# A two-layer encoder on one core: the last down-projection made token-major, with seven half-size products in place of eight

## The chip, the core and the metric

The kernel runs on one core of a Trainium2 chip. The metric is device time in microseconds of one execution, input and output in the chip's memory. The engines named below are PE (TensorE: matmuls), ACT (ScalarE), DVE (VectorE), POOL (GpSimd) and SP (SyncE, which here only issues DMAs). SBUF is the on-chip memory of 128 partitions, PSUM the eight banks into which PE accumulates.

## The reference

A bidirectional encoder trunk of two layers, in float32, on 512 tokens of 1024 channels. Cut to what matters here:

```python
for l in range(DEPTH):                          # DEPTH = 2
    h = rmsnorm(x, g_mix[l])
    proj = h @ w_in[l]                          # gates, conv, three attentions
    ...                                         # four branches, gated and summed
    x = x + mixed @ w_out[l]
    x = x + conv_ffn(rmsnorm(x, g_ffn[l]), w_up[l], ffn_conv_w[l], ffn_conv_b[l], w_down[l])

def conv_ffn(h, w_up, conv_w, conv_b, w_down):
    u = depthwise_conv(h @ w_up, conv_w, conv_b)      # width 3 over the tokens
    gate, up = split(u, 2)                            # 2816 channels each
    return (silu(gate) * up) @ w_down                 # 2816 -> 1024
```

The output is x, 512 tokens by 1024 channels.

## The kernel before

**Products in three parts.** Matmuls run in the type float32r. To keep float32's precision each operand is split into a rounded part (hi) and a rest (lo), and each product is three matmuls, hi x hi, hi x lo and lo x hi, added up in one PSUM bank. A matmul takes a stationary operand of 128 x 128 and a moving one of 128 x 512, and writes 128 x 512, one bank. `prod` issues these three.

**Feature-major.** Mostly activations lie with channels on the partitions and tokens along the row, as blocks of 128 channels by 512 tokens; the weights are the stationary operand. The projections that feed attention are token-major (`token_major`): there the activations are stationary, 128 tokens at a time, and the weights move, 512 columns at a time.

**Weights.** They are packed on the host into units of up to 1024 columns of 128 partitions (512 KB), in order of use (`weight_units`, `pack_weights`). `weights` emits for each unit a DMA on SP's queue into `w_raw` (two buffers), a copy by ACT into `w_hi` and a subtraction by DVE into `w_lo` (three buffers each). `unit` hands out the next one. All instructions are put in order when the program is built: each has a priority, that of its place in the code, weights some 3000 places ahead of theirs, and an engine's queue takes what is ready in that plan, by priority. On the chip every engine then works its queue strictly in order. A buffer that is used again waits until all that used it before is done.

**The feed-forward part.** `ffn` takes 22 block pairs i; for each, two up-projection blocks of 24 matmuls (gate and up), then scaling, the convolution over tokens and the gating on DVE and ACT, in buffers `U0` to `U3`, `cy0`, `cy1` and `fth`, and at its end the split of the block into `fh` and `fl`, which stay. The down-projection then runs over eight output blocks m, each the sum over 22 blocks, with three weight units of 1024, 896 and 896 columns, and `update` adds the residual (`xr`, loaded from memory, to `xn`) and stores it; in the last layer into `outT`, feature-major, which the host transposes. In the first layer `update` also prepares the next layer's normalised input (`norm_tile`), and `finish_norm` starts the row of scales, which goes through memory on POOL's queue.

**PSUM.** Two groups of four banks in rotation, `mm` and `aux`; the feed-forward part uses `mm` alone.

**Memory pools.** `gate`, `attn`, `outp` and `ffn` are opened one after another in each layer and share SBUF; a buffer of a later pool waits for those that lay there before.

Of the kernel before, what the change touches and what calls it, by code (L numbers as in the profile page):

```python
# [14 lines left out]
F32 = mybir.dt.float32  # L15
# [3 lines left out]
ALU = mybir.AluOpType  # L19
# [8 lines left out]
NB = S // P  # L28
DFF = 2816
NF = DFF // P  # L30
EPS = 1e-6
BIG = 1e30
EB = 4
# [29 lines left out]
COL_A, COL_NA, COL_DIL, COL_SWA = 4096, 4608, 5376, 6144  # L63


def weight_units():

    units = []

    tok = lambda *cols: units.extend(('in_t', (cols, k, 2), 1024) for k in range(0, 8, 2))  # L70
    tok((COL_NA, 512))
    tok((COL_NA + 512, 256), (COL_DIL + 512, 256))
    tok((COL_DIL, 512))
    for j in (2, 0, 3, 1):
        units.append(('in_d', COL_A + j * P, 1024))
    tok((COL_SWA, 512))
    for n in ORDER:
        for d in range(8):
            units.append(('in_d', n * D + d * P, 1024))
            if d in (2, 6):  # L80
                units.append(('branch', (n, d // 4), 1024))
    for d in range(8):
        units.append(('out', d, 1024))
    for i in range(NF):
        units.append(('up', i * P, 1024))
        units.append(('up', DFF + i * P, 1024))
    for m in range(8):
# [5 lines left out]
UNITS = weight_units()  # L93
WLEN = sum(u[2] for u in UNITS) * P


def pack_weights(w_in, w_branch, w_out, w_up, w_down):
    out = np.empty((L, WLEN), np.float32)
    for l in range(L):
        off = 0  # L100
        for kind, a, n in UNITS:
            dst = out[l, off:off + n * P]
            off += n * P
            if kind == 'in_t':
                cols, k0, kn = a
                src = np.concatenate([w_in[l][k0 * P:(k0 + kn) * P, c:c + w] for c, w in cols], 1)
                src = src.reshape(kn, P, 512).transpose(1, 0, 2)
            elif kind == 'branch':
                b, h = a
                src = w_branch[l][b].reshape(2, P, 8, P)[:, :, 4 * h:4 * h + 4].transpose(1, 2, 0, 3)  # L110
            elif kind == 'down':
# [73 lines left out]
class Trunk:  # L185
# [7 lines left out]
    def weights(self, upto, ahead=3000, parts=1, queue=None):  # L193

        nc = self.nc
        while self.w_emitted < min(upto, len(self.w_list)):
            l, off, n = self.w_list[self.w_emitted]
            with self.tc.high_priority(offset=ahead):
                raw = self.wpool.tile([P, 1024], F32, name="w_raw", tag="w_raw", bufs=2)
                hi = self.wpool.tile([P, 1024], F32R, name="w_hi", tag="w_hi", bufs=3)  # L200
                lo = self.wpool.tile([P, 1024], F32R, name="w_lo", tag="w_lo", bufs=3)
                src = self.W[l, off:off + n * P].rearrange("(p c) -> p c", p=P)
                for i in range(parts):
                    s = slice(i * n // parts, (i + 1) * n // parts)
                    (queue or nc.sync).dma_start(raw[:, s], src[:, s])
                for i in range(parts):
                    s = slice(i * n // parts, (i + 1) * n // parts)
                    w = nc.scalar.activation(hi[:, s], raw[:, s], AF.Copy)  # L208
                    self.first_hi = self.first_hi or w
                    nc.vector.tensor_tensor(lo[:, s], raw[:, s], hi[:, s].bitcast(F32), ALU.subtract)  # L210
            self.w_ready.append((hi, lo))
            self.w_emitted += 1
# [7 lines left out]
    def mm(self):  # L220
        return self.psum.tile([P, 512], F32, name="mm", tag="mm", bufs=4)
# [610 lines left out]
            self.tick()  # L832


    def update(self, d, ps, pool, last):
# [5 lines left out]
        nc.vector.tensor_tensor(xn, ps, xr, ALU.add)  # L841
        if last:
            nc.sync.dma_start(self.out[d], xn)
        else:
            nc.sync.dma_start(self.xnew[d], xn)
            self.norm_tile(d, xn, pool)
# [5 lines left out]
    def ffn(self):  # L852
        nc = self.nc
        v = nc.vector
        U = []
        for i in range(4):
            u = self.fp.tile([P, 514 + (4 * PHASE if i == 3 else 0)], F32, name=f"U{i}", tag=f"U{i}", bufs=1)
            nc.gpsimd.memset(u[:, 0:1], 0.0)
            nc.gpsimd.memset(u[:, 513:514], 0.0)
            U.append(u)  # L860
        F = []
        for i in range(NF):
            ys, pss = [], []
            for s in range(2):
# [18 lines left out]
            f = ys[1]  # L883
            v.tensor_tensor(f, f, ys[0], ALU.mult)  # L884
            fh = self.fp.tile([P, S], F32R, name=f"fh{i}", tag=f"fh{i}", bufs=1)
            fl = self.fp.tile([P, S], F32R, name=f"fl{i}", tag=f"fl{i}", bufs=1)
            nc.scalar.activation(fh, f, AF.Copy, scale=0.5)  # L887
            v.scalar_tensor_tensor(fl, f, 0.5, fh.bitcast(F32), ALU.mult, ALU.subtract)
            F.append((fh, fl))
        return F  # L890


    def run(self):
        nc, tc = self.nc, self.tc
        with ExitStack() as st:
# [6 lines left out]
            self.dram = pool("dram", space=bass.MemoryType.DRAM)  # L902
            self.w_list = []
            for l in range(L):
                off = 0
                for _, _, n in UNITS:
                    self.w_list.append((l, off, n))
                    off += n * P
            self.w_emitted = self.w_used = 0
            self.first_hi = None  # L910
            self.w_ready = []
# [43 lines left out]
    def layer(self, l):  # L955
# [3 lines left out]
        with tc.tile_pool(name="gate", bufs=1, reuse_waits="tile") as self.gp:  # L959
# [26 lines left out]
            with tc.tile_pool(name="outp", bufs=1, reuse_waits="tile") as self.op:  # L986
# [3 lines left out]
                for d in range(0, KT, 2):  # L990
# [3 lines left out]
                    for k0, k1 in zip(cuts, cuts[1:]):  # L994
                        for e in range(2):
# [5 lines left out]
                                self.prod(pss[e], hi[:, s], lo[:, s], self.MH[k][0], self.MH[k][1], k == 0,  # L1001
                                          k == KT - 1)
                            if k1 == KT:
                                self.update(d + e, pss[e], self.op, False)
                self.xres = self.xnew
                self.finish_norm(1)
        with tc.tile_pool(name="ffn", bufs=1, reuse_waits="tile") as self.fp:
            self.scratch = lambda: self.fp.tile([P, S], F32, name="raw", tag="cy0", bufs=2)
            F = self.ffn()
            if not last:  # L1010
                self.load_prm(l + 1)
                self.xnew = self.new_res()
                self.start_norm('g_mix')
            for m in range(KT):
                ps = self.mm()
                for k0, kn in ((0, 8), (8, 7), (15, 7)):
                    hi, lo = self.unit()
                    for j in range(kn):
                        k = k0 + j
                        s = slice(j * P, (j + 1) * P)  # L1020
                        self.prod(ps, hi[:, s], lo[:, s], F[k][0], F[k][1], k == 0, k == NF - 1)
                self.update(m, ps, self.fp, last)
            if not last:
                self.xres = self.xnew
                self.finish_norm(1, 10)

    def derive_params(self):
        nc = self.nc
# [42 lines left out]
```

## Time and profile before

| | |
|---|---|
| time, median of 3 executions | 1587.83 us (1587.66 to 2181.0) |
| profiled execution | 1587.48 us, its span in the profile 1585.7 us |
| granted PE clock | 1.0 of full speed |
| matmuls | 7298 in the profile |
| first layer's down-projection | about 676 to 794 us |
| second layer's up-projection | about 1227 to 1461 us |
| last down-projection | 1461.7 to 1581.6 us |
| memory traffic | 177.70 MB, 112 GB/s in the mean |

The profile names instructions by line of the kernel, engine and operation, then the output and the inputs by the program's names (`mm<-fh,w_hi` is a matmul into an `mm` bank from these two), shapes, and a count. In the listings by line the figures after the bar are the time busy in all, the mean of one in ns, and the idle time of the engine just before them with what ended it. In the order of time each row starts with the start and the length in us. Times to landing are of a DMA from its issue to its completion. The line numbers are those of the kernel before.

### The profile page before, as it was taken

What the parts mean: (1) busy time and instruction counts of PE and PEld (TensorE: products, weight loads), DVE (VectorE), ACT (ScalarE), POOL (GpSimd) and SP (SyncE); (2) the same over time, 40 slices, a digit from 0 to 9 for tenths busy, and PEclk for the clock granted to TensorE, in tenths of its full rate; (3) what the DMA queues carried; (4) which work ended last, traced back from release to release, by engine and by line L of the source; (5) the groups of instructions that cost most, each with busy time, mean ns of one, the idle gap of its engine ahead of it and who ended that gap; (6) DMA issues with size and microseconds to landing.
All of it is one profiled execution on the core that took longest, in us unless ns stands there. A gap on an engine that the chain in (4) does not pass through costs nothing.

```text
span 1585.7 us, 19717 instructions
## 1 busy us (share of the span) xinstructions
PE 1579.1 (100%) x7298; PEld 1314.2 (83%) x7298; DVE 1103.3 (70%) x1847; ACT 782.0 (49%) x1334; POOL 105.6 (7%) x176
## 2 busy tenths in 40 slices
PE   9999999999999999999999999999999999999998
PEld 8888888888888888888888888888888888888887
DVE  6689888755578787743356898887556787787221
ACT  6778777243444444422247687763334444444221
POOL 0102001221000000000002020021210000000000
PEclk9999999999999999999999999999999999999999
DMA  6622222222532222234345312222326222222332
GB/s 236 184 97 89 85 80 76 98 100 98 183 118 98 102 93 94 103 118 139 118 157 174 111 68 86 79 86 90 104 94 211 93 107 99 94 94 101 123 130 71
DMA packets 60080, 177.70 MB, mean 112 GB/s; under 512 B 7120, under 2 KB 9040, under 8 KB 59984
## 3 DMA queue, kind: packets, MB, share of 16 engines
q1 hardware_dynamic: 59248, 174.87, 32.6%
q0 software_dynamic: 448, 1.06, 0.3%
q8 instruction: 57, 0.93, 0.2%
q10 hardware_dynamic: 288, 0.52, 0.1%
q14 instruction: 39, 0.32, 0.1%
HBM read 160.68 MB, written 10.49 MB: 108 GB/s over the span
## 4 chain that ended last, share of the span: by engine, by line
PE 94%; DVE 3%; ACT 3%; issue 0%; DMA 0%; SPq 0%; ACTq 0%; DVEq 0%
PE mm L231 26%; PE mm L229 26%; PE mm L230 26%; PE mm L423 2%; PE mm L425 2%; PE mm L424 2%; PE aux L695 2%; PE aux L424 1%; PE aux L425 1%; PE aux L423 1%; PE aux L657 1%; PE aux L658 1%; PE aux L719 1%; DVE w_lo L210 1%; ACT w_hi L208 1%; PE aux L722 0%
## 5 line engine op out<-in xcount | busy, mean ns | idle before, releaser
L229 PE MATMUL mm<-xh,w_hi 128*128 128x512 f32 x1280 | 499.9, 391 | 0.0
L231 PE MATMUL mm<-xh,w_lo 128*128 128x512 f32 x1280 | 499.0, 390 | 0.0
L230 PE MATMUL mm<-xl,w_hi 128*128 128x512 f32 x1280 | 498.5, 389 | 0.0
L208 ACT ACTIVATE w_hi<-w_raw 128x1024 fp32r<-128x1024 f32 (+2 forms) x273 | 284.4, 1042 | 400.3 <-PE mm L230 330.8
L210 DVE TENSOR_TENSOR w_lo<-w_raw,w_hi 128x1024 fp32r<-128x1024 f32 (+2 forms) x273 | 329.4, 1207 | 146.0 <-ACT w_hi L208 142.2
L231 PEld LDWEIGHTS mm<-xh,w_lo 128*128 128x128 f32 x1280 | 240.3, 188 | 51.1
L230 PEld LDWEIGHTS mm<-xl,w_hi 128*128 128x128 f32 x1280 | 240.4, 188 | 48.9
L229 PEld LDWEIGHTS mm<-xh,w_hi 128*128 128x128 f32 x1280 | 240.3, 188 | 48.2
L230 PE MATMUL mm<-fl,w_hi 128*128 128x512 f32 x352 | 136.9, 389 | 0.0
L229 PE MATMUL mm<-fh,w_hi 128*128 128x512 f32 x352 | 136.9, 389 | 0.0
L231 PE MATMUL mm<-fh,w_lo 128*128 128x512 f32 x352 | 136.9, 389 | 0.0
L799 POOL TENSOR_TENSOR mx<-mx,t 128x512 f32<-128x512 f32 x44 | 66.9, 1529 | 429.0 <-DVE t L798 327.6
L361 DVE SCALAR_TENSOR_TENSOR cv<-cv,prm 128x512 f32<-128x512 f32 x120 | 93.8, 782 | 0.7
L887 ACT ACTIVATE fh<-cy 128x512 fp32r<-128x512 f32 x44 | 27.8, 632 | 112.1 <-DVE cy L884 112.1
L841 DVE TENSOR_TENSOR xn<-mm,xr 128x512 f32<-128x512 f32 x32 | 22.1, 691 | 84.3 <-PE mm L231 63.9
L875 ACT ACTIVATE cy<-U,prm 128x512 f32<-128x512 f32 x88 | 71.2, 811 | 13.5 <-DVE U L872 12.5
L230 PEld LDWEIGHTS mm<-fl,w_hi 128*128 128x128 f32 x352 | 66.1, 188 | 13.8
L229 PEld LDWEIGHTS mm<-fh,w_hi 128*128 128x128 f32 x352 | 66.1, 188 | 13.8
L769 DVE TENSOR_TENSOR t<-mm,RB 128x512 f32<-128x512 f32 x64 | 44.0, 688 | 47.9 <-PE mm L231 47.2
L231 PEld LDWEIGHTS mm<-fh,w_lo 128*128 128x128 f32 x352 | 66.1, 188 | 13.5
L423 PE MATMUL mm<-w_hi,xh 128*128 128x512 f32 x192 | 76.4, 398 | 0.4 <-DVE V L553 0.4
L872 DVE TENSOR_TENSOR U<-mm,RB 128x512 f32<-128x512 f32 x88 | 60.4, 688 | 22.8 <-PE mm L231 14.6
(152 smaller groups left out, 2266.6 us busy)
## 6 DMA issues: line engine op xcount, KB each, us to landing
w_raw<-W SPq DMA_DIRECT2D x239, 512.0 KB, 3.5
w_raw<-W SPq DMA_DIRECT2D x32, 448.0 KB, 3.3
res<-xn SPq DMA_DIRECT2D x24, 256.0 KB, 2.0
xr<-res SPq DMA_DIRECT2D x24, 256.0 KB, 2.9
KH<-KH SPq DMA_DIRECT2D x20, 128.0 KB, 3.4
KL<-KL SPq DMA_DIRECT2D x20, 128.0 KB, 3.9
mx<-TB SPq DMA_DIRECT2D x8, 256.0 KB, 4.8
turn<-pt SPq DMA_DIRECT2D x16, 128.0 KB, 2.5
```

The lines of the kernel that those rows point to most:

```text
L208: w = nc.scalar.activation(hi[:, s], raw[:, s], AF.Copy)
L210: nc.vector.tensor_tensor(lo[:, s], raw[:, s], hi[:, s].bitcast(F32), ALU.subtract)
L229: mm(ps, lhsT=wh, rhs=xh, start=start, stop=False)
L230: mm(ps, lhsT=wh, rhs=xl, start=False, stop=False)
L231: self.last_mm = mm(ps, lhsT=wl, rhs=xh, start=False, stop=stop)
L361: self.after_mm(v.scalar_tensor_tensor(acc, u[:, t:t + S], w(t), acc, ALU.mult, ALU.add))
L423: mm(pss[b], lhsT=self.Xh[k][:, t], rhs=hi[:, s], start=k == 0, stop=False)
L424: mm(pss[b], lhsT=self.Xh[k][:, t], rhs=lo[:, s], start=False, stop=False)
L425: self.last_mm = mm(pss[b], lhsT=self.Xl[k][:, t], rhs=hi[:, s], start=False, stop=k == KT - 1)
L799: (v if n == ORDER[3] and d >= 6 else nc.gpsimd).tensor_tensor(m, m, t, ALU.add)
L872: v.tensor_tensor(u[:, 1:513], ps, self.RB, ALU.mult)
L875: nc.scalar.activation(y, u[:, 1:513], AF.Identity, scale=w(1), bias=self.par('ffn_conv_b', c))
```

## The change

The last layer's down-projection is computed token-major, as four blocks of 128 tokens by two halves of 512 output columns.

- The first six of the 22 channel blocks (`NK`) are plain products, with weight units of two blocks by 512 columns.
- The other sixteen make eight pairs (`NP2`). Over them, tokens, output columns and channels are each halved (the two blocks of a pair are the two channel halves), and the 2 x 2 by 2 x 2 block product is taken by the Winograd form of Strassen's scheme: seven products of half size in place of eight, of sums of activation blocks (`s1` to `s4`, `a11`, `a12`, `a22`) with sums of weight blocks (`t1` to `t3` and one more) or with weight blocks themselves. Four products (A, B, C, E) run together over the eight pairs; their results are combined; and the last three are accumulated onto the banks of A, C and E.
- The weight sums are made in the first layer's down-projection: `weight_sums(j)`, after each output block, loads four blocks of 128 x 512 on POOL's queue, takes four differences on DVE and stores four sums to memory on POOL's queue.
- The activation sums, and their splits into hi and lo, are made by `split_pair` on DVE and ACT, during the plain part and the first products. `ffn` leaves the last sixteen blocks unsplit for it.
- The residual is turned to token-major in the second layer's `ffn`: `turn_res(d)` loads a block, transposes it in 32 x 32 squares on DVE and stores it in four DMAs to `resT`; it is read back as `xt`, which takes up the products and is stored to `out`.
- The last part has 34 weight units in place of 24. The units of the seven products come from the packed weights and from the sums, mostly as two DMAs of 256 KB, and every other one of them is loaded into a third raw buffer, `w_more`.

```diff
+    def last_units(self):
+        more = lambda f: self.w_list.append((0, f))
+        quad = lambda j, q: self.quads[j][:, q * S:(q + 1) * S]
+        sums = lambda j, a, b: self.sums[j][:, a * S:b * S]
+        for j in range(NP2):
+            more(lambda j=j: [quad(j, 0), sums(j, 0, 1)])
+            self.w_list.append((1024, lambda j=j: [sums(j, 1, 3)]))
+        for f in (lambda j: quad(j, 2), lambda j: quad(j, 3), lambda j: sums(j, 3, 4)):
+            for j in range(0, NP2, 2):
+                g = lambda f=f, j=j: [f(j), f(j + 1)]
+                more(g) if j % 4 else self.w_list.append((1024, g))
 ...
     def weights(...):
+                if n == 0:
+                    n = 1024
+                    raw = self.fp.tile([P, 1024], F32, name="w_raw", tag="w_more", bufs=1)
 ...
+    def weight_sums(self, j):
+        b11, b12, b21, b22 = bs = [... tag=f"U{i}" ...]
+        for q in range(4):
+            nc.gpsimd.dma_start(bs[q], self.quads[j][:, q * S:(q + 1) * S])
+        v.tensor_tensor(t3, b22, b12, ALU.subtract)
+        v.tensor_tensor(b12, b12, b11, ALU.subtract)
+        v.tensor_tensor(t2, b22, b12, ALU.subtract)
+        v.tensor_tensor(b21, b21, t2, ALU.subtract)
+        for n, t in enumerate((t2, b12, t3, b21)):
+            nc.gpsimd.dma_start(self.sums[j][:, n * S:(n + 1) * S], t)
 ...
+    def turn_res(self, d):
+        nc.sync.dma_start(xr, self.xres[d])
+        nc.vector.transpose(xn, xr)
+        rows = self.resT.rearrange("(i a) c -> a i c", a=32)
+        for q in range(4):
+            nc.sync.dma_start(rows[:, :, d * P + 32 * q:d * P + 32 * q + 32],
+                              xn[32 * q:32 * q + 32].rearrange("a (i b) -> a i b", b=32))
 ...
+    def split_pair(self, F, j, got):
+        def split(h, l, x):
+            nc.scalar.activation(h, x, AF.Copy)
+            v.tensor_tensor(l, x, h.bitcast(F32), ALU.subtract)
+        v.tensor_tensor(a[:, lo], fi[:, hi], fk[:, hi], ALU.add)
+        v.tensor_tensor(fi[:, hi], fi[:, lo], fi[:, hi], ALU.subtract)
+        v.tensor_tensor(a[:, hi], a[:, lo], fi[:, lo], ALU.subtract)
+        split(ih, il, fi)
+        split(ah, al, a)
+        split(kh, kl, fk)
+        v.tensor_tensor(fk[:, lo], fk[:, lo], a[:, hi], ALU.subtract)
+        split(bh, bl, fk[:, lo])
 ...
+    def last_down(self, F):
+        for h in range(2):                       # the plain part
+            pss = [(self.mm if h == 0 else self.aux)() for _ in range(NB)]
+            ...
+            for k0 in range(0, NK, 2):
+                w = self.unit()
+                for b, k in ([(b, k) for b in range(NB) for k in range(2)] if k0 + 2 == NK else
+                             [(b, k) for k in range(2) for b in range(NB)]):
+                    prod(pss[b], [f[:, t] for f in F[k0 + k]], w, k, k0 + k == 0, k0 + k == NK - 1)
+                    if k0 + k == NK - 1:
+                        v.tensor_tensor(xt[b, h], pss[b], xt[b, h], ALU.add)
+                if todo:
+                    self.split_pair(F, todo.pop(0), got)
+        A, B = ([self.mm() for _ in range(2)] for _ in range(2))
+        C, E = ([self.aux() for _ in range(2)] for _ in range(2))
+        for j in range(NP2):                     # four products together
+            ...
+            for ops in (((A, 'a11', 0), (B, 's2', 1)), ((C, 's1', 0), (E, 's3', 1))):
+                w = self.unit()
+                for banks, x, c in ops:
+                    for b in range(2):
+                        prod(banks[b], got[j][x][b], w, c, j == 0, j == NP2 - 1)
+        ...                                      # A copied by ACT, adds on DVE
+        for banks, x, n, h in ((A, 'a12', 0, 0), (C, 's4', 0, 1), (E, 'a22', 2, 0)):
+            for j in range(0, NP2 - 4, 2):
+                w = self.unit()
+                ...
+            ws = [self.unit() for _ in range(2)]
+            for b in range(2):
+                for j in range(NP2 - 4, NP2):
+                    prod(banks[b], got[j][x][b], ws[(j - NP2 + 4) // 2], j % 2, False, j == NP2 - 1, True)
+                v.tensor_tensor(xt[n + b, h], xt[n + b, h], banks[b], ALU.add)
+                self.store(xt, n + b, h)
```

More of the change, by code (lines that the diff above doesn't have):

```diff
@@ L30 @@
 NF = DFF // P
+NP2 = 8
+NK = NF - 2 * NP2
 EPS = 1e-6
@@ L86, in weight_units @@
         units.append(('up', DFF + i * P, 1024))
+    if last:
+        units.extend(('rows', (k0, h), 1024) for h in range(2) for k0 in range(0, NK, 2))
+        units.extend(('quad', NK + 2 * j, 2048) for j in range(NP2))
+        return units
     for m in range(8):
@@ L90, in weight_units @@
     return units
-UNITS = weight_units()
-WLEN = sum(u[2] for u in UNITS) * P
+UNITS = [weight_units(l == L - 1) for l in range(L)]
+WLEN = max(sum(u[2] for u in us) for us in UNITS) * P
 def pack_weights(w_in, w_branch, w_out, w_up, w_down):
-    out = np.empty((L, WLEN), np.float32)
+    out = np.zeros((L, WLEN), np.float32)
     for l in range(L):
         off = 0
-        for kind, a, n in UNITS:
+        for kind, a, n in UNITS[l]:
             dst = out[l, off:off + n * P]
@@ L110, in pack_weights @@
                 src = w_branch[l][b].reshape(2, P, 8, P)[:, :, 4 * h:4 * h + 4].transpose(1, 2, 0, 3)
+            elif kind == 'rows':
+                k0, h = a
+                src = w_down[l][k0 * P:(k0 + 2) * P, h * 512:(h + 1) * 512].reshape(2, P, 512).transpose(1, 0, 2)
+            elif kind == 'quad':
+                src = w_down[l][a * P:(a + 2) * P].reshape(2, P, 1024).transpose(1, 0, 2)
             elif kind == 'down':
@@ L196, in weights @@
         while self.w_emitted < min(upto, len(self.w_list)):
-            l, off, n = self.w_list[self.w_emitted]
+            n, pieces = self.w_list[self.w_emitted]
             with self.tc.high_priority(offset=ahead):
-                raw = self.wpool.tile([P, 1024], F32, name="w_raw", tag="w_raw", bufs=2)
+                if n == 0:
+                    n = 1024
+                    raw = self.fp.tile([P, 1024], F32, name="w_raw", tag="w_more", bufs=1)
+                else:
+                    raw = self.wpool.tile([P, 1024], F32, name="w_raw", tag="w_raw", bufs=2)
                 hi = self.wpool.tile([P, 1024], F32R, name="w_hi", tag="w_hi", bufs=3)
                 lo = self.wpool.tile([P, 1024], F32R, name="w_lo", tag="w_lo", bufs=3)
[L202 to L205, printed above, removed]
+                src = pieces()
+                if len(src) == 1:
+                    cut = [slice(i * n // parts, (i + 1) * n // parts) for i in range(parts)]
+                    src = [src[0][:, s] for s in cut]
+                c = 0
+                for p in src:
+                    (queue or nc.sync).dma_start(raw[:, c:c + p.shape[1]], p)
+                    c += p.shape[1]
                 for i in range(parts):
@@ L832, in finish, with update @@
             self.tick()
-    def update(self, d, ps, pool, last):
+    def update(self, d, ps, pool):
         nc = self.nc
@@ L841, in update, with ffn @@
         nc.vector.tensor_tensor(xn, ps, xr, ALU.add)
[L842 to L846, printed above, removed]
+        nc.sync.dma_start(self.xnew[d], xn)
+        self.norm_tile(d, xn, pool)
     def new_res(self):
         return [self.dram.tile([P, S], F32, name=f"res{d}", tag=f"res{d}", bufs=2) for d in range(KT)]
-    def ffn(self):
+    def ffn(self, last):
         nc = self.nc
@@ L883, in ffn @@
             f = ys[1]
+            fh = self.fp.tile([P, S], F32R, name=f"fh{i}", tag=f"fh{i}", bufs=1)
+            late = last and i >= NK
+            fl = self.fp.tile([P, S], F32 if late else F32R, name=f"fl{i}", tag=f"fl{i}", bufs=1)
+            if last and i % 2 == 1 and i // 2 < KT:
+                self.turn_res(i // 2)
+            if late:
+                v.scalar_tensor_tensor(fl, ys[0], 0.5, f, ALU.mult, ALU.mult)
+                F.append((fh, fl))
+                continue
             v.tensor_tensor(f, f, ys[0], ALU.mult)
-            fh = self.fp.tile([P, S], F32R, name=f"fh{i}", tag=f"fh{i}", bufs=1)
-            fl = self.fp.tile([P, S], F32R, name=f"fl{i}", tag=f"fl{i}", bufs=1)
             nc.scalar.activation(fh, f, AF.Copy, scale=0.5)
@@ new lines, in weight_sums @@
+    def weight_sums(self, j):
+        nc = self.nc
+        v = nc.vector
+        b11, b12, b21, b22 = bs = [self.fp.tile([P, 514 + (4 * PHASE if i == 3 else 0)], F32, name=f"U{i}",
+                                                tag=f"U{i}", bufs=1)[:, :S] for i in range(4)]
+        for q in range(4):
+            nc.gpsimd.dma_start(bs[q], self.quads[j][:, q * S:(q + 1) * S])
+        t3 = self.fp.tile([P, S], F32, name="cy0", tag="cy0", bufs=2)
+        t2 = self.fp.tile([P, S], F32, name="cy1", tag="cy1", bufs=2)
+        v.tensor_tensor(t3, b22, b12, ALU.subtract)
+        v.tensor_tensor(b12, b12, b11, ALU.subtract)
+        v.tensor_tensor(t2, b22, b12, ALU.subtract)
+        v.tensor_tensor(b21, b21, t2, ALU.subtract)
+        self.sums[j] = self.dram.tile([P, 4 * S], F32, name=f"sums{j}", tag=f"sums{j}", bufs=1)
+        for n, t in enumerate((t2, b12, t3, b21)):
+            nc.gpsimd.dma_start(self.sums[j][:, n * S:(n + 1) * S], t)
@@ L893, in run, with store @@
+    def store(self, xt, b, h):
+        self.nc.sync.dma_start(self.out[b * P:(b + 1) * P, h * S:(h + 1) * S], xt[b, h])
     def run(self):
@@ L1003, in layer @@
                             if k1 == KT:
-                                self.update(d + e, pss[e], self.op, False)
+                                self.update(d + e, pss[e], self.op)
                 self.xres = self.xnew
                 self.finish_norm(1)
+        if last:
+            self.resT = self.dram.tile([S, D], F32, name="resT", tag="resT", bufs=1)
         with tc.tile_pool(name="ffn", bufs=1, reuse_waits="tile") as self.fp:
             self.scratch = lambda: self.fp.tile([P, S], F32, name="raw", tag="cy0", bufs=2)
[L1009 to L1013, printed above, removed]
+            F = self.ffn(last)
+            if last:
+                self.last_down(F)
+                return
+            self.load_prm(l + 1)
+            self.xnew = self.new_res()
+            self.start_norm('g_mix')
+            self.sums = [None] * NP2
             for m in range(KT):
@@ L1021, in layer @@
                         self.prod(ps, hi[:, s], lo[:, s], F[k][0], F[k][1], k == 0, k == NF - 1)
[L1022 to L1025, printed above, removed]
+                self.update(m, ps, self.fp)
+                if m < NP2:
+                    self.weight_sums(m)
+            self.xres = self.xnew
+            self.finish_norm(1, 10)
     def derive_params(self):
@@ L1065 @@
     args = [nc.dram_tensor(k, a.shape, F32, kind="ExternalInput").ap() for k, a in arrays.items()]
-    out = nc.dram_tensor("outT", (KT, P, S), F32, kind="ExternalOutput").ap()
+    out = nc.dram_tensor("out", (S, D), F32, kind="ExternalOutput").ap()
     with _tile.TileContext(nc) as tc:
@@ L1069 @@
     r = _run(nc, [arrays], core_ids=[0])
-    return np.ascontiguousarray(np.asarray(r.results[0]["outT"]).reshape(D, S).T).reshape(1, S, D)
+    return np.asarray(r.results[0]["out"]).reshape(1, S, D)
```

72 lines of the change are left out of this document (68 added, 4 removed).

## The prediction

> **What bounds the kernel now.** I read the busy shares first, then the chain that ended last, then the stages.
>
> ```profile
> PE 1579.1 (100%) x7298; PEld 1314.2 (83%) x7298; DVE 1103.3 (70%) x1847; ACT 782.0 (49%) x1334; POOL 105.6 (7%) x176
> PE 94%; DVE 3%; ACT 3%; issue 0%; DMA 0%; SPq 0%; ACTq 0%; DVEq 0%
> 0.00:20.00 20.00, 18.55 (x80) 15.67 (x81) 14.74 (x26) 14.83 (x22) 0.44 (x8) 1.00 0.81 276
> 676.00:797.00 121.00, 121.00 (x535) 100.24 (x534) 46.79 (x67) 34.54 (x42) 0.31 (x4) 1.00 0.39 129
> 1227.00:1461.00 234.00, 234.00 (x1038) 193.94 (x1037) 184.62 (x248) 105.52 (x130) 1.13 (x2) 1.00 0.28 99
> 1461.70:1582.00 120.30, 119.87 (x529) 98.95 (x527) 33.70 (x35) 23.15 (x24) 0.00 (x0) 1.00 0.32 109
> ```
>
> TensorE (PE) is busy all the time and 94% of the chain. The four window rows give length, then busy time of PE, its weight loads, DVE, ACT and POOL, then granted clock (1.00 throughout), DMA share and GB/s: the kernel's first 20 us, the first layer's down-projection, the second layer's up-projection, and the stage that changes. There DVE works 34 us of 120 and moves 109 GB/s; nothing but PE is near a limit. So the change is worth what it takes from PE, less any new PE wait.
>
> The price of a matmul is not its duration. Its instructions by tile, and two in a token-major stage:
>
> ```profile
> L229 PE MATMUL mm<-fh,w_hi x176: 389/389/390, 1461.7 to 1580.7; 128*128 128x512 f32 x176
> L231 PE MATMUL mm<-fh,w_lo x176: 388/389/390, 1462.2 to 1581.2; 128*128 128x512 f32 x176
> ...
> 803.19 0.39 PE L423 MATMUL aux<-w_hi,xh 128*128 128x512 f32 x1
> ...
> 815.43 0.39 PE L423 MATMUL aux<-w_hi,xh 128*128 128x512 f32 x1
> ```
>
> 389 ns is how long one takes from start to end, but they overlap. From the first L229 to the last lie 175 groups of three: (1580.7 - 1461.7) / 525 = 0.2267 us each. Token-major (activations as the stationary operand, weights moving) there are 54 steps between the two rows: 12.24 / 54 = 0.2267, the same. 48 x 389 ns would overstate the gain by 70%.
>
> **What PE saves.** Before: 8 output blocks x 22 x 3 = 528 matmuls. After: six blocks plain, 2 halves x 6 x 4 token blocks x 3 = 144; seven products, each 8 pairs x 2 token blocks x 3 = 48, so 336; together 480. All have 512 columns. Saved: 48 x 0.2267 = **10.9 us**. Nothing is added on PE: the residual is turned on DVE and by DMA, the sums are DVE's.
>
> **The end** stays. The last matmul is followed by one DVE add and one 256 KB store, as now:
>
> ```profile
> 1581.60 0.69 DVE L841 TENSOR_TENSOR xn<-mm,xr 128x512 f32<-128x512 f32 x1 [13.11 <-PE mm L231]
> 1582.32 0.34 SPq L843 DMA_DIRECT2D outT<-xn  x1
> ```
>
> **What must keep up: the weight units.** A unit of 1024 columns is loaded by SP's queue into w_raw, copied by ACT to w_hi, subtracted by DVE to w_lo; the raw buffer is then free, and the next load goes.
>
> ```profile
> L210 DVE TENSOR_TENSOR w_lo<-w_raw,w_hi 128x1024 fp32r<-128x1024 f32 x239 | 293.1, 1227 | 97.9 <-ACT w_hi L208 95.4
> L208 ACT ACTIVATE w_hi<-w_raw 128x1024 fp32r<-128x1024 f32 x239 | 252.6, 1057 | 291.1 <-PE mm L230 223.0 <-issue 36.9 <-PE mm L425 16.1
> 1477.69 1.09 DVE L210 TENSOR_TENSOR w_lo<-w_raw,w_hi 128x896 fp32r<-128x896 f32 x1
> 1478.82 0.33 SPq L205 DMA_DIRECT2D w_raw<-W  x1
> DMA to landing us min/median/max: 3.1/3.4/4.2
> DMA to landing us min/median/max: 2.7/2.8/2.9
> w_raw<-W SPq DMA_DIRECT2D x7, 512.0 KB, 4.2
> w_raw<-W SPq DMA_DIRECT2D x2, 512.0 KB, 4.7
> DMA to landing us min/median/max: 2.9/3.5/5.9
> ```
>
> The split costs 1.06 + 1.23 us; the load is issued 0.04 us after the subtraction ends (1478.78 to 1478.82). The landings: w_raw in the last stage; 256 KB of xr in the first down-projection; w_raw in 400 to 435 us; w_raw in 8 to 12 us, when the queues are fullest; w_raw over the whole span.
>
> Now a unit feeds 21 to 24 matmuls, 4.8 to 5.4 us. It still feeds 24 in the plain part (6 units, 32.6 us), but in the seven products only 12: **2.72 us**, for 28 units (76.2 us). There 512 KB per 2.72 us is 193 GB/s, under the 276 of the first row, but the buffers matter. Every other of these units goes through w_more, one buffer, so that one cycle of it must fit in two units, 5.44 us. The cycle: 0.04 to the issue, some 0.45 until its second 256 KB is issued, that one's landing, 1.06 + 1.23 and about 0.05 between them. With the 2.8 us of xr it is 5.6 us; with 3.2, which I take since 193 GB/s lies above the 129 beside that row, 6.0; and some 0.15 for a DVE and an ACT that now have other work in their queues: **6.15**, 0.7 over. What protects PE: w_hi and w_lo have three buffers, so a unit's buffer is free two units, 5.44 us, before its use, and the split takes 2.4: 3.0 us of slack. In the first 16 units (8 through w_more, 7 gaps) 7 x 0.7 = 4.9 us fall behind, 1.9 beyond the slack. Two w_raw units then follow each other, so that the gap is three units, 8.16 us, and gives 2.0 back; five gaps of the last twelve take 3.5, and holding two units at once for the last four pairs frees one buffer 1.4 us late: some 2.5 more. In all PE waits **4.4 us**. Bounds: nothing at 2.8 us (5.6 is 0.15 over, 1.1 in 7 gaps, under 3.0); at the first row's 4.2 for the second half (cycle 7.15, 1.7 over) 7 x 1.7 - 3.0 = 9 and 5 x 1.7 + 1.4 - 1.0 = 9, so 18.
>
> A sentence by itself: the Trainium skill's page "DMA: Bandwidth & Descriptors" (Anatomy of one DMA) gives 2.0 us and bytes over 436 GB/s, measured from GpSimd's queue, so 2.6 us for 256 KB by estimate; by it the cycle would be 5.4 and PE would wait for nothing, 1576.6, while the rows stand 0.2 above it. Its section on latency puts access to the memory at 2 us under high load, which speaks for the slower end.
>
> **DVE, the second limit.**
>
> ```profile
> L884 DVE TENSOR_TENSOR cy<-cy,cy 128x512 f32<-128x512 f32 x44 | 30.4, 691 | 1.4
> L703 DVE TENSOR_TENSOR pt<-aux,pt 128x256 fp32r<-128x256 f32 x48 | 20.1, 419 | 1.0 <-ACT pt L702 0.6
> L888 DVE SCALAR_TENSOR_TENSOR fl<-cy,fh 128x512 fp32r<-128x512 f32 x44 | 30.5, 692 | 28.0 <-ACT fh L887 27.9
> L887 ACT ACTIVATE fh<-cy 128x512 fp32r<-128x512 f32 x44 | 27.8, 632 | 112.1 <-DVE cy L884 112.1
> L702 ACT ACTIVATE pt<-aux 128x256 fp32r<-128x256 f32 x48 | 18.1, 377 | 2.9 <-PE aux L695 2.2 <-DMA V<-turn 0.2
> ```
>
> split_pair has five operations of 256 columns and three of 512 on DVE: 5 x 0.42 + 3 x 0.69 = 4.2 us, eight times 33.4. Before the last pair is used (312 matmuls, 70.7 us into the stage) DVE also has 20 w_lo (24.5), eight adds from the banks (5.5) and 2.9 left of the last up block: 66.3 of 70.7 us. It fits with 4.4 us to spare, but each subtraction may wait 0.7 us for ACT, as L888 does; with one such wait per pair, 5.6 us, PE would be held 1.2 us. It is not added: the waits on the loads give DVE that time. If w_lo did not fill those waits it would cost up to 7. At the switch to the seven products the aux banks must be emptied by adds queued behind the splits: up to 2 us, again in place of a later load wait. I take 0 for both and 9 as the upper end. ACT has 34 x 1.06 for the units and 8 x (3 x 0.63 + 0.38) for the pairs, 54 us of 109.
>
> **What is hidden.** The removed half of the splits in the second up-projection (16 x 0.69 us DVE, 16 x 0.63 ACT) lies under PE: 0. turn_res: eight transposes, no row, by L884 about 0.7 us; 185 of 234 us were busy, and 11 go: 0, at most 6 if PE had to wait for all of them. Its SP instructions (one load, four stores) stand ahead of weight loads; a unit there has 5.4 us and five units are ahead (three split, two raw), so a store that waits for the transpose may hold SP 10 us without effect. weight_sums: 32 x 0.69 = 22 us on DVE, busy 47 of 121; 64 DMAs on POOL's queue, idle there; 16.8 MB in 120 us add 140 GB/s to 129, 269 where 276 was reached. Loads land later, but a unit of 5.4 us against a landing even of 5.9 leaves over 2 us: 0. The next layer then opens tables in that memory on SP:
>
> ```profile
> 796.39 0.33 SPq L205 DMA_DIRECT2D w_raw<-W  x1
> 796.77 0.42 SPq L597 DMA_DIRECT2D mx<-TB  x1
> ```
>
> If the last weight sums are made only after the last update, these wait for 2.8 us of DVE and a store, about 7 us, and the weights behind them too; the five units ahead cover it: 0, else 2. The norm's row on POOL, behind the last stores, is needed after three projections of 96 matmuls, 65 us later: 0.
>
> **Sum.** The profiled execution took 1587.48 us (span 1585.7 and 1.8 around it; the median shown is 0.35 higher). 1587.5 - 10.9 + 4.4 = **1581.0**.
>
> **Rivals.**
> 1. *Nothing waits.* The loads land in 2.8 us or the w_raw buffers run ahead far enough: 1587.5 - 10.9 = 1576.6. For it: 109 GB/s now, and 3.4 us for twice the bytes. Against: a single w_more. 0.28.
> 2. *The w_more chain takes more than is saved* (the other side). Place: the 28 half-length units. From a cycle of about 6.65 us (second half landing in 3.7) PE waits 7 x 1.2 - 3.0 and then 5 x 1.2 - 1.5 + 1.4, 11 us, all of the gain; at 4.2, 18 us: 1595. For it: the 4.2 and 4.7 rows. Against: those stretches had several transfers at once, here there are about two. 0.15.
> 3. *DVE, not the loads, holds PE*: subtractions idle behind ACT, adds behind splits, 9 us: 1585.6. For it: 66 of 70.7 us. Against: w_lo and the adds can fill the gaps. 0.12.
> 4. *The turning of the residual clogs SP.* Each turn stores 2048 pieces of 128 bytes; no row has such. Nearest, 512 pieces of 2 KB:
>
> ```profile
> V<-turn SPq DMA_DIRECT2D x2, 1024.0 KB, 7.0
> ```
>
> By count, four stores of 512 pieces are at most 28 us per 21.8 us of two up blocks; then loads lag 6 us each turn, 50 in all, less 18 of cover: 1608. By bytes a store is a sixteenth of that row. 0.03. The Trainium skill, same page (Specifications), wants pieces of 512 bytes for full rate and says that smaller ones are read and rewritten: that speaks for it, and no run shown has such pieces.
>
> That the change does not do what it says is excluded by the count of matmuls in the code.
>
> **How the numbers follow.** My forecast, a part of the gain lost: 0.42; the rivals 0.28, 0.15, 0.12, 0.03. The range runs from just under nothing lost (1576) past rival 3 and a mild rival 2 to 1592, leaving out the rest of 2 and 4. About 2% (32 us) is what a measurement here tells from no change: 10.9 us is the whole gain, so faster by that is 0.01; slower needs 43 us of waits: 0.02; within it 0.97.
>
> **What would show it.** 480 matmuls in the last stage at 0.2267 us; the stage near 113 us, not 120. PE idle behind w_lo or w_hi of units that came through w_more, growing from the middle of the first sixteen; ACT's w_hi waiting for DMA, not for PE. Rival 1: no such idle. Rival 3: PE waits released by split tiles or banks. Rival 4: PE idle in the second up-projection. I am wrong if PE idles in the first layer, or the landing of 256 KB under 193 GB/s lies outside 2.8 to 3.7 us.

## The result, and the profile after

The changed kernel takes 1609.59 us (median of 4, 1607.74 to 1612.38) against 1587.74 us: a ratio of 1.014, 95% interval 1.012 to 1.0159. It is 22 us slower, where 1581 was predicted and 1592 was the top of the range. The profiled execution has a span of 1610.3 us, 24.6 longer than before. The page, with its fortieth parts of the span (from here on a line number is that of the kernel that ran; in the changed one L225 is SP's issue of a weight load, shown as SPq, L229 is ACT's copy, L231 DVE's subtraction, L250 to L252 and L1006 to L1008 are the three matmuls of a product):

```profile
PE 1581.7 (98%) x7250; PEld 1310.1 (81%) x7250; DVE 1167.6 (73%) x1963; ACT 798.6 (50%) x1362; POOL 140.8 (9%) x240
...
PE   9999999999999999997999999999999999999998
...
PEclk9999999999999999998999999999999999999999
...
PE 82%; DMA 6%; DVE 5%; ACT 3%; issue 2%; POOL 1%; SPq 0%; ACTq 0%; DVEq 0%; POOLq 0%
```

PE has 48 matmuls less and is busy longer. In the chain of waits it falls from 94% to 82%, DMA rises from 0 to 6%, DVE from 3 to 5%, and POOL appears. The first hole is in the 19th slice, about 725 to 765 us: not in the stage that was rewritten but in the first layer's down-projection, where the weight sums are made. Windows over the two down-projections, the last layer's first (length, PE, weight loads, DVE, ACT, POOL, clock, DMA share, GB/s):

```profile
1485.10:1606.40 121.30, 114.59 (x481) 91.25 (x479) 82.40 (x123) 45.98 (x59) 0.00 (x0) 0.97 0.46 151
675.10:817.40 142.30, 126.73 (x529) 102.69 (x528) 65.04 (x96) 33.69 (x40) 33.58 (x65) 0.94 0.66 222
```

528 matmuls at 0.2267 us are 119.7 us, 480 are 108.8. So the first layer's stage lost 142.3 - 119.7 = **22.6 us**, and the last one 121.3 - 108.8 = **12.5 us** where 4.4 were forecast. The sum closes: 22.6 + 12.5 - 10.9 is 24.2 of the 24.6. Between the two stages little moved: the first matmul of the last stage comes 23.4 us later than before, 22.6 of them from the first layer. In neither stage is the clock 1.00.

Whom PE waited for, in the whole run:

```profile
PE mm L252 <- DVE w_lo L231: 15.6, 5, 5.8
PE aux L1006 <- ACT w_hi L229: 2.6, 1, 2.6
PE mm L1007 <- DVE w_lo L231: 2.2, 4, 0.8
...
PE mm L1006 <- ACT w_hi L229: 1.1, 1, 1.1
PE aux L1007 <- DVE w_lo L231: 0.7, 1, 0.7
```

L252 is the feature-major product, here that of the first layer: five waits, 15.6 us. The other rows are the last stage, 6.6 us. All are for weight units. Why w_lo is late in the first layer stands in DVE's own waits from 676 to 820 us, and in DVE's order of time around the longest but one of PE's five waits:

```profile
DVE cy L959 <- DMA U<-W: 49.7, 8, 8.0
```

```profile
722.41 0.69 DVE L959 TENSOR_TENSOR cy<-U,U 128x512 f32<-128x512 f32 x1 [6.82 <-DMA U<-W]
...
724.47 1.22 DVE L231 TENSOR_TENSOR w_lo<-w_raw,w_hi 128x1024 fp32r<-128x1024 f32 x1
```

```profile
725.74 0.80 PE L252 MATMUL mm<-fh,w_lo 128*128 128x512 f32 x1 [5.10 <-DVE w_lo L231]
```

L959 is the first subtraction of weight_sums. Each of the eight stands at the head of DVE's queue until its blocks have come through POOL's queue, 49.7 us in all; w_lo is queued behind it, and PE waits for that w_lo: 5.1 us here.

The last stage shows the chain that was forecast. The chain of waits from 1560 us on, with the load that goes through w_more, its copy and its subtraction, and then the next load:

```profile
1560.14 0.33 SPq L225
...
1560.51 3.71 DMA w_raw<-W
...
1564.33 1.07 ACT w_hi L229
...
1565.42 1.24 DVE w_lo L231
1566.67 0.33 SPq L225
...
1570.78 1.07 ACT w_hi L229
...
1573.12 0.33 SPq L225
...
1577.64 1.07 ACT w_hi L229
...
1579.99 0.33 SPq L225
...
1585.68 1.06 ACT w_hi L229
```

A cycle is 6.53, 6.45 and 6.87 us from issue to issue, where 6.15 was taken and two units last 5.44. At its end PE waits 2.6 us and, one matmul later, 0.7, and the six us behind that pass at a granted clock of 0.51. DVE was full earlier, from 1505 to 1520 us, where PE did not wait:

```profile
1588.00:1594.00 6.00, 5.95 (x14) 4.70 (x15) 1.81 (x2) 0.86 (x1) 0.00 (x0) 0.51 0.44 131
```

```profile
1505.00:1520.00 15.00, 15.00 (x67) 12.41 (x67) 15.00 (x29) 6.84 (x11) 0.00 (x0) 1.00 0.34 106
```

### The profile page after: what moved, and what is told of

The parts are those of the page before. It is cut to its first block, busy times and chain, and to the rows that moved or that the text cites. A ratio compares the mean times of both kernels' runs of the same rounds, so it can differ in the third digit from the quotient of the medians.

```text
span 1610.3 us, 20056 instructions
## 1 busy us (share of the span) xinstructions
PE 1581.7 (98%) x7250; PEld 1310.1 (81%) x7250; DVE 1167.6 (73%) x1963; ACT 798.6 (50%) x1362; POOL 140.8 (9%) x240
## 4 chain that ended last, share of the span: by engine, by line
PE 82%; DMA 6%; DVE 5%; ACT 3%; issue 2%; POOL 1%; SPq 0%; ACTq 0%; DVEq 0%; POOLq 0%
PE mm L252 22%; PE mm L250 22%; PE mm L251 22%; DMA U<-W 3%; PE mm L444 2%; PE mm L446 2%; PE mm L445 2%; DVE w_lo L231 2%; PE aux L716 2%; ACT w_hi L229 1%; DMA w_raw<-sums 1%; DMA w_raw<-W 1%; PE aux L445 1%; PE aux L446 1%; DMA sums<-U 1%
## 5 line engine op out<-in xcount | busy, mean ns | idle before, releaser
L250 PE MATMUL mm<-xh,w_hi 128*128 128x512 f32 x1280 | 499.9, 391 | 0.0
L252 PE MATMUL mm<-xh,w_lo 128*128 128x512 f32 x1280 | 499.0, 390 | 0.0
L229 ACT ACTIVATE w_hi<-w_raw 128x1024 fp32r<-128x1024 f32 (+2 forms) x283 | 295.5, 1047 | 402.9 <-PE mm L251 219.8
L231 DVE TENSOR_TENSOR w_lo<-w_raw,w_hi 128x1024 fp32r<-128x1024 f32 (+2 forms) x283 | 342.7, 1214 | 94.6 <-ACT w_hi L229 89.5
L252 PEld LDWEIGHTS mm<-xh,w_lo 128*128 128x128 f32 x1280 | 240.2, 188 | 51.1
L250 PEld LDWEIGHTS mm<-xh,w_hi 128*128 128x128 f32 x1280 | 240.3, 188 | 48.2
L252 PE MATMUL mm<-fh,w_lo 128*128 128x512 f32 x176 | 71.6, 407 | 15.6 <-DVE w_lo L231 15.6
L446 PE MATMUL mm<-w_hi,xl 128*128 128x512 f32 x192 | 75.0, 392 | 0.0
L445 PE MATMUL mm<-w_lo,xh 128*128 128x512 f32 x192 | 74.9, 390 | 0.0
L250 PE MATMUL mm<-fh,w_hi 128*128 128x512 f32 x176 | 70.6, 401 | 0.0
L251 PE MATMUL mm<-fl,w_hi 128*128 128x512 f32 x176 | 70.4, 400 | 0.0
L703 ACT ACTIVATE e<-e,rl 128x256 f32<-128x256 f32 (+2 forms) x96 | 57.4, 598 | 23.8 <-DVE rl L702 23.5
L895 DVE SCALAR_TENSOR_TENSOR cy<-U,prm,cy 128x512 f32<-128x512 f32 x88 | 65.9, 750 | 2.7
L894 DVE SCALAR_TENSOR_TENSOR cy<-U,prm,cy 128x512 f32<-128x512 f32 x88 | 65.5, 746 | 2.0 <-ACT cy L893 2.0
```

What stands on the lines that cost most here:

```text
L250: mm(ps, lhsT=wh, rhs=xh, start=start, stop=False)
L251: mm(ps, lhsT=wh, rhs=xl, start=False, stop=False)
L252: self.last_mm = mm(ps, lhsT=wl, rhs=xh, start=False, stop=stop)
L445: mm(pss[b], lhsT=self.Xh[k][:, t], rhs=lo[:, s], start=False, stop=False)
L446: self.last_mm = mm(pss[b], lhsT=self.Xl[k][:, t], rhs=hi[:, s], start=False, stop=k == KT - 1)
```

## The experiments

**1. No weight sums at all.** The kernel leaves out `weight_sums`; the units take plain weight blocks in place of sums.

```diff
-        sums = lambda j, a, b: self.sums[j][:, a * S:b * S]
+        sums = lambda j, a, b: self.quads[j][:, a * S:b * S]
...
-                if m < NP2:
-                    self.weight_sums(m)
```

> Leaves out the making of the weight sums: in the first layer nothing is loaded, subtracted or stored, and the last stage loads plain weight blocks in place of the sums, so the output is not the reference's. All theories: the first layer's down-projection falls from 142.4 us back to about 120 (before: 119.7), and the last stage, which is untouched, keeps its 121 us, 12.5 above 480 matmuls. Total about 1609.6 - 22.7 = 1587. If the last stage also gets shorter, the two parts are not independent.

Measured: 1587.76 us (1586.15 to 1590.15), ratio 1.0001 (0.9991 to 1.001). The stage of the first layer is whole again, and the last one still lost 11 us:

```profile
676.00:797.00 121.00, 121.00 (x536) 100.19 (x535) 46.79 (x66) 34.91 (x42) 0.31 (x4) 1.00 0.40 129
1461.90:1581.90 120.00, 114.65 (x482) 91.84 (x480) 82.65 (x124) 46.27 (x60) 0.00 (x0) 0.97 0.47 153
```

The last stage loses its 11 us without the first one's loss, and alone gives back just what its 48 matmuls save.

**2. The transfers without the subtractions.** The kernel leaves out the four differences and stores blocks as they are.

```diff
-        v.tensor_tensor(t3, b22, b12, ALU.subtract)
-        v.tensor_tensor(b12, b12, b11, ALU.subtract)
-        v.tensor_tensor(t2, b22, b12, ALU.subtract)
-        v.tensor_tensor(b21, b21, t2, ALU.subtract)
...
-        for n, t in enumerate((t2, b12, t3, b21)):
+        for n, t in enumerate((b22, b12, b11, b21)):
```

> All loads and stores of the weight sums stay, the four subtractions on DVE are left out (the blocks are stored as they are, so the output is not the reference's). Theory A, a subtraction that waits for POOL's load stands at the head of DVE's queue and w_lo stands behind it: first down-projection about 120 us, total 1587 to 1589. Theory B, the 16.8 MB of added transfers make the weight units land late by themselves: it stays near 140, total 1605 to 1610.

Measured: 1587.19 us, ratio 0.9998 (0.9989 to 1.0008).

```profile
676.00:797.00 121.00, 121.00 (x536) 100.20 (x535) 46.70 (x66) 34.59 (x42) 32.49 (x63) 1.00 0.78 259
...
w_raw<-W SPq DMA_DIRECT2D x14, 448.0 KB, 5.2
w_raw<-W SPq DMA_DIRECT2D x11, 512.0 KB, 4.2
```

259 GB/s run beside the matmuls, the weight units land in 5.2 and 4.2 us where they take 3.3 and 3.4 in the same stage of experiment 1, and PE never waits there. Theory B falls: the added traffic is felt, and hidden.

**3. The same subtractions on POOL.**

```diff
-        v.tensor_tensor(t3, b22, b12, ALU.subtract)
+        nc.gpsimd.tensor_tensor(t3, b22, b12, ALU.subtract)
...
```

> The four subtractions of weight_sums are made by POOL in place of DVE; transfers and results are the same. Theory A: DVE never waits for these loads, first down-projection 120 to 122 us, total 1587 to 1590. Theory B: still near 140 us, total 1605 to 1610. POOL takes some 1.5 us each (its adds in the trace of before), 49 us in all, and waits itself for the loads, so the sums may be done later than now, which costs nothing by either theory.

Measured: 1589.41 us (1586.16 to 1592.34), ratio 1.0011 (1.0001 to 1.002).

```profile
676.00:797.00 121.00, 121.00 (x535) 100.22 (x535) 61.37 (x66) 34.86 (x42) 73.82 (x87) 1.00 0.75 253
1463.50:1581.00 117.50, 111.62 (x481) 89.30 (x479) 82.49 (x123) 46.00 (x59) 0.00 (x0) 1.00 0.49 156
```

With all transfers and all sums, and only the wait taken from DVE's queue to POOL's, the first stage runs full. Theory A holds so far. The last stage keeps a clock of 1.00 here and takes 117.5 us: the chain through w_more by itself, without a fallen clock, costs 8.7 us.

**4. Two w_more buffers.**

```diff
-                    raw = self.fp.tile([P, 1024], F32, name="w_raw", tag="w_more", bufs=1)
+                    raw = self.fp.tile([P, 1024], F32, name="w_raw", tag="w_more", bufs=2)
...
-        xn = self.fp.tile([P, S], F32, name="xn", tag="xn", bufs=2)
+        spare = ("s4h6", "s4l6")[d % 2]
+        xn = self.fp.tile([P, S], F32, name="xn", tag=spare, bufs=1)
...
-        u = [self.fp.tile([P, S], F32, name="xn", tag="xn", bufs=2) for _ in range(2)]
+        u = [self.fp.tile([P, S], F32, name="fth", tag="fth", bufs=2) for _ in range(2)]
```

> w_more gets two buffers in place of one (room is made by letting turn_res write into buffers of split_pair that are idle then). Theory C, one cycle of the single w_more, 6.3 to 6.9 us, against the 5.44 us of two units, holds PE in the last stage: the stage falls from 121 us to 109 to 111, total about 1598. Theory D, DVE, busy all the time from 1490 to 1520 us, holds it, or the three buffers of w_hi and w_lo: the stage stays above 117, total 1606 to 1610. First layer unchanged by both.

Measured: 1600.87 us, ratio 1.0082 (1.0067 to 1.0097).

```profile
1487.50:1596.00 108.50, 108.50 (x480) 89.85 (x479) 82.80 (x123) 46.69 (x59) 0.00 (x0) 1.00 0.51 165
```

Whom ACT's copy waited for, in the changed kernel from 1440 us on and here from 1487 to 1600:

```profile
ACT w_hi L229 <- DMA w_raw<-sums: 20.1, 6, 4.7
ACT w_hi L229 <- DMA w_raw<-W: 17.0, 4, 6.0
```

```profile
ACT w_hi L229 <- PE mm L1009: 20.8, 12, 3.6
ACT w_hi L229 <- PE aux L1009: 17.6, 10, 3.1
```

480 matmuls in 108.5 us, no idle time, clock 1.00, and ACT waits for PE to free w_hi where it had waited for the loads. Theory C holds and D falls: DVE, with 82.8 us of work here, was not the limit. The first layer's stage is disturbed as in the changed kernel, so the total is 1601.

**5. Both repairs: POOL's sums and two w_more buffers.**

> Both repairs together: the weight sums subtracted by POOL, and two w_more buffers. If the two losses are all there is, the first down-projection takes 119.5 us as in the run with POOL, the last stage 108.8 as in the run with two buffers, and the total is that of before less the 48 matmuls: 1587.7 - 10.9 = 1576.8, within 1 us. A third loss would show as 1580 or more.

Measured: 1577.91 us (1576.84 to 1578.7), ratio 0.9938 (0.9925 to 0.9951). No third loss of a size that shows.

**6. DVE's sums, placed later in its queue.** With two w_more buffers as in 4.

```diff
-        v.tensor_tensor(t3, b22, b12, ALU.subtract)
...                                            # all four
+        for ins in (v.tensor_tensor(t3, b22, b12, ALU.subtract),
...
+            self.after_mm(ins)
```

`after_mm` puts an instruction behind the last matmul so far when the queues are planned; on the chip it adds no wait.

> The subtractions go back to DVE, but each is placed in its queue behind the last matmul of its output block (a planning dependency as the convolution has it); two w_more buffers. If the place in DVE's queue is what cost, and not DVE's 22 us of work: first down-projection 120 to 122 us, total 1577 to 1579. The loads of a pair take about 15 us from the stores of the last one, as long as a block, so that DVE may wait about 1 us each. If DVE's work itself is what cost: over 130 us, total 1588 or more.

Measured: **1576.85 us** (1576.76 to 1577.79), ratio 0.9932 (0.9919 to 0.9945), the best of all. The window of the first layer's stage, and DVE's longest wait for the loads there:

```profile
676.00:797.00 121.00, 121.00 (x536) 100.19 (x535) 65.65 (x95) 34.66 (x42) 31.56 (x58) 1.00 0.77 254
```

```profile
DVE cy L960 <- DMA U<-W: 15.5, 7, 2.8
```

DVE does the same 22 us of sums, and PE waits for none of it. So the loss was the place in the queue. The waits are longer than I expected, 2.2 us each and not 1, but the units already split cover them; in the changed kernel they were 49.7 us in eight.

**7 and 8. What a wait costs.** In the changed kernel's first stage PE idled 15.6 us, and 22.6 were lost. To price a wait by itself, the kernel before was given three, ahead of output blocks 2, 4 and 6 of its last stage:

```diff
-                ps = self.mm()
+                old, ps = (ps if m else None), self.mm()
+                if last and m in (2, 4, 6):
+                    z = self.fp.tile([P, S], F32, name="fth", tag="fth", bufs=2)
+                    self.nc.vector.tensor_tensor(z, old, self.RB, ALU.mult)
+                    for _ in range(1):                       # 7 in the long one
+                        self.nc.vector.tensor_tensor(z, z, z, ALU.add)
+                    self.nc.tensor.matmul(ps[:, 0:1], lhsT=z[:, :P], rhs=self.cst[:, C_ONE:C_ONE + 1],
+                                          start=True, stop=True)
```

> The kernel before, with three added waits: ahead of output blocks 2, 4 and 6 of the last down-projection one extra matmul of one column reads the end of a chain of two DVE operations on the block just finished, and PE waits for it. The wait is about 0.5 + 2 x 0.7 + 0.2, 2 us each, 6 us in all. Theory E, a wait costs its own length: 1594. Theory F, a wait also lowers the granted clock for some us afterwards: more, but at 2 us not or little: 1594 to 1596.

> The same with chains of eight DVE operations: waits of about 6.3 us, 19 us in all. Theory E: 1607, and matmuls at 0.227 us right behind each wait. Theory F: matmuls at up to 0.43 us for some 5 us behind each wait, as behind the longest one of the changed kernel, 2 to 3 us more for each: 1613 to 1616, and a granted clock below 1.0 in those stretches.

Measured: 1603.65 us with the short waits (ratio 1.0105, 1.0089 to 1.0121), 1619.55 with the long ones (1.02, 1.0185 to 1.0214). PE's idle time at the added matmul (in all, times, longest), first the short, then the long; they are longer than meant:

```profile
PE mm L1021 <- DVE fth L1020: 9.0, 3, 3.1
```

```profile
PE mm L1021 <- DVE fth L1020: 22.1, 3, 7.4
```

15.9 us were lost with the short ones (14.8 in the profiled run, which has the 9.0 of idling), and 31.8 with the long ones for 22.1. Behind a long wait, in order of time and in windows:

```profile
1500.30 0.63 PE L230 MATMUL mm<-fl,w_hi 128*128 128x512 f32 x1
...
1504.56 0.44 PE L231 MATMUL mm<-fh,w_lo 128*128 128x512 f32 x1
```

```profile
1499.00:1504.50 5.50, 5.23 (x13) 4.23 (x14) 0.22 (x1) 0.00 (x0) 0.00 (x0) 0.50 0.01 3
1504.50:1510.00 5.50, 5.50 (x25) 4.52 (x24) 1.23 (x1) 1.06 (x1) 0.00 (x0) 0.99 0.00 0
```

From 1500.30 to 1504.56 ten matmuls start 0.427 us apart, at a granted clock of 0.50; then it is back. Against steps of 0.2267 us, 2.6 us are lost behind this wait and 2.9 and 3.0 behind the other two, 8.6 of the 9.7 us beyond the idling; the rest is the step into each wait and the added matmuls. The short waits are mixed:

```profile
1495.00:1500.00 5.00, 5.00 (x24) 4.14 (x25) 0.00 (x0) 0.00 (x0) 0.00 (x0) 1.00 0.38 109
1529.00:1534.40 5.40, 5.40 (x13) 4.18 (x14) 0.00 (x0) 0.00 (x0) 0.00 (x0) 0.50 0.24 85
1565.00:1568.40 3.40, 3.40 (x10) 2.68 (x10) 0.00 (x0) 0.00 (x0) 0.00 (x0) 0.54 0.51 141
```

These are the stretches behind three waits of 3.0 to 3.1 us: after one the clock stayed, after two it halved, for 5 and 3 us. Theory E falls, F holds, and at 3 us the length of the wait does not decide. Shorter waits can do it too. In the last stage of experiment 1 two waits of 0.9 and 0.8 us, with one matmul between them, were enough (the order of time, then a window behind them):

```profile
1530.07 0.50 PE L1006 MATMUL mm<-w_hi,fh 128*128 128x512 f32 x1 [0.89 <-ACT w_hi L229]
1531.33 0.51 PE L1007 MATMUL mm<-w_lo,fh 128*128 128x512 f32 x1 [0.76 <-DVE w_lo L231]
...
1531.70:1535.00 3.30, 3.30 (x9) 2.56 (x8) 0.71 (x1) 0.00 (x0) 0.00 (x0) 0.50 0.66 188
```

In experiment 3 a pair of 1.9 and 0.8 us was followed by a clock of 1.00. The Trainium skill's page "TensorE: Matmul & The Clock Gate" (Part 1) has the rule: a free-running window of about 3.4 us, half rate after an idle one, full rate after a busy one. The traces agree on the half rate, 0.50 granted and at most some 5 us of it; they differ on the idle window, since waits of 3.0 us and even the pair above are shorter than it, and there the measurement decides. What decides among such short waits is not shown.

It fits the changed kernel too: three of its five waits in the first stage were long, 5.1 us above and these two (its order of time, and its waits from 775 to 800 us),

```profile
750.46 0.79 PE L252 MATMUL mm<-fh,w_lo 128*128 128x512 f32 x1 [5.79 <-DVE w_lo L231]
```

```profile
PE mm L252 <- DVE w_lo L231: 2.9, 1, 2.9
```

and a window behind the last of them shows the clock:

```profile
778.30:781.20 2.90, 2.90 (x8) 2.26 (x7) 2.90 (x5) 1.25 (x2) 1.05 (x2) 0.50 0.99 350
```

7.0 us went beyond the idling. By the order of time 2.4, 1.9 and 1.7 of them, 6.0 us in all, were lost behind these three waits, against steps of 0.2267 us.

## Why the prediction was wrong

Wrong in sign, and outside its range; only the 0.97 for a change of less than 2% held. Both signs that it named for being wrong came: PE idled in the first layer, and loads of 256 KB in the last stage, 3.5 to 3.7 us in the median, took up to 5.2 where 3.7 was the bound.

- **What PE saves: right.** 480 matmuls at 0.2267 us, 108.5 us in experiment 4; with both losses gone the kernel is 10.9 us faster than before (1576.85 against 1587.79 in the same runs), the forecast gain to the tenth. Taking the step between starts, and not the 389 ns of one, was what made that number.
- **What is hidden: the step that failed.** weight_sums was put at 0, by DVE's occupancy ("32 x 0.69 = 22 us on DVE, busy 47 of 121") and by the landing of the weights. Both were true, as experiments 2 and 6 show, and neither was the question. The subtraction is an instruction that *waits*, for a load through another queue; the prediction did not ask what is queued behind it on DVE. There stood w_lo, on which PE depends: DVE waited 49.7 us there, PE waited 15.6 for the w_lo behind, and 7.0 more went with these waits, mostly by the clock. One set of four blocks serves all pairs, so that a load goes only when the stores of the pair before have landed, and then it takes its time:

```profile
U<-W POOLq DMA_DIRECT2D x32, 256.0 KB, 5.4
```

- **The w_more chain: right mechanism, mis-sized.** Forecast 6.15 us per cycle and 4.4 us of waiting; measured 6.45 to 6.87, and 12.5 us lost. (By the prediction's own figures the second part of the 4.4 is 3.5 + 1.4 - 2.0 = 2.9 and not 2.5, so 4.8 in all; that is small beside the miss.) In the first sixteen units about 4 us were lost where 1.9 was forecast, in the last twelve 8.5 where 2.5 was. What the cycle lacked is the load: from its issue to the copy 4.1 to 4.5 us (1560.14 to 1564.33 and the two after it; 5.7 the last time) where 0.45 + 3.2 was taken. The clock, which no term had, took 2.8 of the 12.5 behind the longest wait; with a clock of 1.00, in experiment 3, 8.7 were lost, still about twice the forecast. Rival 2 happened, with a chance of 0.15 on it. That its price from a cycle of 6.65 us on, 11 us, lies so near the 12.5 is in part luck, since it holds no clock. And it is not what made the kernel 1.4% slower: alone it ends at 1587.8.
- **DVE as the second limit: not met.** It was busy 15.0 of 15 us from 1505 to 1520, as the 66 of 70.7 us promised, and experiment 4 shows PE without a wait on it.
- **The turning of the residual: hidden, as forecast.** In the second layer's up-projection PE was busy all the time at a clock of 1.00, so rival 4 did not come. The eight transposes took 0.70 us each, the 0.7 estimated; xr landed in 2.6 to 5.5 us there, 3.9 in the median, where 2.7 to 2.9 was seen in the first down-projection of before.
- **The end and the switch to the seven products: 0, as taken.** No wait for a bank shows among PE's waits.

## What to carry to other kernels

Work that is added "beside" the bound engine cost here by what it waited for, not by its busy time: ask which instructions stand behind it in that engine's queue, and whether the bound engine needs them. Move the wait to a queue in which nothing urgent stands, or place the instruction where its data has long landed. A rotation of buffers is as slow as its scarcest member: here one buffer in every second place cost the whole gain of this change, and a second one brought it back.

## What the runs showed of the hardware beyond the expected

A wait of PE can cost more than its length, through a granted clock of 0.50 behind it: 1.7 to 3.0 us on top in the stretches above. The clock fell behind all eight waits of 3.7 us and more in these runs (5.1 and 5.8 us in the changed kernel, 3.7, 4.9 and 5.7 in experiment 4, three of 7.3 to 7.4 with the long waits), behind some of 2.6 to 3.1 us, and behind some pairs of shorter ones, the shortest of 0.9 and 0.8.

POOL's arithmetic slows DVE's. In experiment 5, with the subtractions on POOL, the same DVE operation in the first layer's stage takes longer than in experiment 6 (first 5, then 6; busy, mean in ns):

```profile
L306 DVE SCALAR_TENSOR_TENSOR xl<-xn,prm,xh 128x512 fp32r<-128x512 f32 x8 | 13.2, 1646 | 0.0
```

```profile
L306 DVE SCALAR_TENSOR_TENSOR xl<-xn,prm,xh 128x512 fp32r<-128x512 f32 x8 | 6.0, 745 | 0.0
```

1646 against 745 ns, both inputs in SBUF. The Trainium skill's page "SBUF — State Buffer" (Who interferes with whom) says that a DVE instruction with two inputs in SBUF contends with a POOL instruction that reads SBUF; the traces agree.
